# Two-layer encoder trunk: stored MLP operands converted three products behind their load at the seam of the two MLP products, and at most 22 halves in advance

## The chip, the cores and the metric

The kernel runs on one core of a Trainium2 chip. The metric is the device time of one execution in microseconds. TensorE multiplies, ScalarE (ACT) and VectorE (DVE) prepare operands and read results out of PSUM, GpSimd (POOL) does little here, SyncE (SP) issues most of the loads, and 16 DMA engines move the data.

## What is computed

Two layers on 1024 tokens of width 1024, in float32: a recurrent mixer and an MLP, then a shared key and value, chunked attention and a second MLP. The change touches the two MLPs:

```python
def sqrelu_mlp(hn, w1, w2):
    return jnp.square(jax.nn.relu(hn @ w1)) @ w2
...
    for layer in range(DEPTH):
...
        hn = modulate(rms_norm(h, norm2_g[layer]), sh2, sc2)
        h = h + g2[:, None, :] * sqrelu_mlp(hn, mlp_w1[layer], mlp_w2[layer])
```

`w1` is 1024 x 4096, `w2` is 4096 x 1024.

## The kernel before

**Precision.** Each float32 operand is split into a high and a low part of a faster type. ScalarE copies the high part (L204), VectorE subtracts it to get the low part (L208). Each tile product is three matmuls, high by high, high by low and low by high (L337 to L339).

**Seven products for eight.** Most of an MLP is done in blocks of 2 by 2 with seven block products instead of eight (the names B11, T1, T2, B22, B21, T3, T4 in `PROD`, numbered x = 0 to 6). The operands are sums of blocks. For the weights VectorE builds them from a loaded *quad* of tiles (L123), after which ScalarE and VectorE convert them. For the hidden activations the sums are built once (L1224) and all blocks are stored to DRAM (`hid`), from where the second product loads them again. One such *piece* holds two blocks of 128 x 512. Each block, once split into high and low, fills one tile and is called a half here; a name needs four of them for the four row groups that a pair of steps uses.

One product of `Quads.product` is 12 matmuls. x = 2 and 5 and 6 add onto the bank that x = 0 began, x = 3 onto that of x = 1. The bank has to be read before it is added to again. In the first product x = 0 to 2 are read by ScalarE (L1306), x = 3 to 5 by VectorE (L1308), x = 6 by ScalarE (L1235). In the second product all are read by VectorE (L1335).

**Order.** In the MLPs and their neighbourhood the order of each engine's instructions is the order in which the Python code issues them. `Stream` (the object `ws`) keeps the books. After the matmuls of a product come, in this order: the read, `flush` (low parts of conversions, at most four units, a half being one and a wide weight tile two), `after` (jobs that are due, changes of limits), then the clock `now` goes up by one and `pump` runs. `pump` first issues loads, as long as the number of *raw* tiles (loaded, not yet converted) is below `ns`. Then it takes the first item of each queue that is ready: "p" builds the sums of a quad, "w" converts weights, "a" converts stored pieces. With `early` set, the raw count falls as soon as the high part is issued. The low part is held back until the next `flush`, so that it stands behind the next read on VectorE. Seven raw tiles come from a ring (`ws`), the others from the 38 general tiles (`s`). A load physically starts when the engine that last used its tile is done with it. With `strict` set, sums of a quad first empty all held-back low parts.

An item is ready when `now` is at least `lag[kind]` past the value at which its load was issued and when its halves still fit: `live` halves plus the new one must not exceed `cap`. For "a", `live` falls by two after each product of every second step of the second product.

**The seam.** The first product ends with the row groups 14 and 15 done as a pair, the second begins with its steps s0 and s1 as a pair. The last product of a pair is carried into the next one. The products around the seam are numbered P0, P1, ... here; (15,0) is row group 15, x = 0:

| P | product | P | product | P | product | P | product |
|---|---|---|---|---|---|---|---|
| 0 | (14,0) | 8 | (15,3) | 16 | (15,6) | 24 | (s0,5) |
| 1 | (14,1) | 9 | (14,4) | 17 | (s1,0) | 25 | (s1,4) |
| 2 | (13,6) | 10 | (14,5) | 18 | (s1,1) | 26 | (s1,5) |
| 3 | (15,0) | 11 | (15,4) | 19 | (s0,2) | 27 | (s0,6) |
| 4 | (15,1) | 12 | (15,5) | 20 | (s0,3) | 28 | (s2,0) |
| 5 | (14,2) | 13 | (14,6) | 21 | (s1,2) | 29 | (s2,1) |
| 6 | (14,3) | 14 | (s0,0) | 22 | (s1,3) | 30 | (s1,6) |
| 7 | (15,2) | 15 | (s0,1) | 23 | (s0,4) | 31 | (s3,0) |

In the load order stand the pieces of B11 for row groups 0 to 3, the two weight quads of s0 and s1 (W0, W1), the pieces of T1, T2, B22, B21, T3 and T4 for the same row groups, B11 to B22 for groups 4 and 5, the quads of s2 and s3 (W2, W3), and so on. W3.0 is the first operand made from the quad W3. `reload` brings back the residual stream in between.

At P3 (row group 15, x = 0) the code sets `lag["p"]` to 2, at each product of group 15 it raises `cap["a"]`, and `ns` becomes 10 (L1317 to L1321). At P14 `lag["p"]` goes back to 4 (L1373, L1374), at P30 `ns` becomes 11 and `strict` ends (L1375, L1376). `lag["a"]` is 2 from the start of the program. `cap["a"]` keeps its last value until the end of the MLP. Layer 0 and layer 1 run the same code.

Of the kernel before, what the change touches and what calls it, by code (L numbers as in the profile page):

```python
# [311 lines left out]
def trunk(ctx: ExitStack, tc: tile.TileContext, I, out, dbg=None, stop=None):  # L312
# [12 lines left out]
    def slot(dt=F32, tag="a", shape=(128, 1024)):  # L325
        cnt[0] += 1
        return ap_.tile(list(shape), dt, name=f"s{cnt[0]}", tag=tag)
# [5 lines left out]
    def hs(half):  # L333
        return slice(half * HALF, (half + 1) * HALF)
# [29 lines left out]
    ws = Stream(nc, slot, whp, wsp)  # L364
# [839 lines left out]
    def mlp_body(l, h, nrm, nxt, last):  # L1204
        g2 = mods[l][:, 40:48]

        def store(p, ca, cb_):

            f = "p (a b) -> p a b"

            def squares():
                if l == 0 and p in (0, 1, 14, 15):
                    nc.scalar.dma_start(hid[p][:, 0:8:7], ca.rearrange(f, a=2))
                else:
                    nc.scalar.dma_start(hid[p][:, 0:1], ca[:, hs(0)].unsqueeze(1))
                nc.scalar.dma_start(hid[p][:, 3:5], cb_.rearrange(f, a=2))

            def sums():
                a, b = hs(0), hs(1)
                for out, in0, in1 in ((cb_[:, a], ca[:, b], cb_[:, a]),  # L1220
                                      (ca[:, b], ca[:, b], ca[:, a]),
                                      (ca[:, a], ca[:, a], cb_[:, a]),
                                      (cb_[:, b], cb_[:, b], ca[:, a])):
                    V.tensor_tensor(out=out, in0=in0, in1=in1, op=ALU.subtract)  # L1224

            def rest_():
                nc.scalar.dma_start(hid[p][:, 1:3], ca.rearrange(f, a=2))
                nc.scalar.dma_start(hid[p][:, 5:7], cb_.rearrange(f, a=2))

            for d, job in zip({12: (2, 3, 4), 13: (2, 3, 4), 14: (2, 16, 20), 15: (6, 18, 22)}.get(p, (2, 4, 8)),  # L1230
                              (squares, sums, rest_)):
                ws.at(d, job)

        def relu2(t, src=None):
            A_.activation(out=t, in_=t if src is None else src, func=AF.Relu)  # L1235
            A_.activation(out=t, in_=t, func=AF.Square)
# [53 lines left out]
        def reload(*ks):  # L1290
            for k in ks:
                h[k] = slot()
                nc.sync.dma_start(h[k], nrm.dram[k])
# [4 lines left out]
        def hidden(p):  # L1298
            ca, cb_ = slot(), slot()
            spots = (ca[:, hs(0)], cb_[:, hs(0)], ca[:, hs(1)], ca[:, hs(1)], ca[:, hs(0)],  # L1300
                     cb_[:, hs(0)], cb_[:, hs(1)])

            def read(x, ps, spots=spots):
                t = spots[x]
                if x < 3:
                    A_.activation(out=t, in_=ps, func=AF.Copy)  # L1306
                elif x < 6:
                    V.tensor_tensor(out=t, in0=t, in1=ps, op=ALU.add)  # L1308
                    ws.at(1, relu2, t)
                else:  # L1310
                    relu2(t, ps)

            def after(x, p=p, ca=ca, cb_=cb_):
                ws.run()
                if x == 6:
                    store(p, ca, cb_)
                if (p, x) == (15, 0):  # L1317
                    ws.lag["p"] = 2
                if p == 15:
                    ws.cap["a"] = min(24, 4 * x + 4)  # L1320
                    ws.ns = 10  # L1321
                    if x in (3, 5):
                        reload(x - 3, x - 2)

            return [ws.next() for _ in range(4)], 4, nrm.op, read, after
# [7 lines left out]
        def add(m, half, ps):  # L1333
            t = h[m][:, hs(half)]
            V.scalar_tensor_tensor(out=t, in0=ps, scalar=g2[:, m : m + 1], in1=t, op0=ALU.mult,  # L1335
                                   op1=ALU.add)
# [3 lines left out]
        def final():  # L1340
            while finals:
                m, half = finals.pop(0)
                if last is not None:
                    last(h, (m,), half)
                else:
                    nxt.sq(m, hs(half))
# [12 lines left out]
        def second(s):  # L1359
            m1, m2 = 2 * (s % 4), 2 * (s % 4) + 1  # L1360
            spots = ((m1, 0), (m2, 1), (m1, 1), (m1, 1), (m1, 0), (m2, 1), (m2, 0))

            def read(x, ps):
                final()
                add(*spots[x], ps)
                if s > 11 and x > 2:
                    finals.append(spots[x])

            def after(x):
                ws.run()  # L1370
                if x == 3 and s < 2:
                    reload(4 + 2 * s, 5 + 2 * s)
                if (s, x) == (0, 0):  # L1373
                    ws.lag["p"] = 4  # L1374
                if (s, x) == (1, 6):  # L1375
                    ws.ns, ws.strict = 11, False  # L1376
                if s == 14 and l == 0:
                    ws.live["a"] -= 4 * (NAMES[x][0] == "T")
                elif s % 2:
                    ws.live["a"] -= 2 if s < 14 else 4  # L1380

            return [ws.next() for _ in range(4)], 4, Operands(s // 2 * 2), read, after
# [483 lines left out]
```

## Time and profile before

| | us |
|---|---|
| median of 3 runs | 2317.44 (2315.03 to 2317.73) |
| profiled execution, its own time | 2313.97 |
| span of that execution | 2312.2 |
| MLP of layer 0: first and last L1308 or L1335 of it | about 526 to 1110 |
| MLP of layer 1 | about 1700 to 2312 |

The granted clock of TensorE is 0.997 over the span. A row of a group or a timeline names the source line, the engine, the operation, output and input, the size and the count. In the timeline the first number is the start from the span's beginning, the second the duration, and a bracket holds how long the engine stood idle before it and who released it. A row of the stretches gives the stretch, its length, the busy time of TensorE, its weight loads, VectorE, ScalarE and GpSimd, each with a count, then the granted clock, the share of the DMA engines and GB/s. Matmul ends are modelled, so the starts are the better measure.

### The profile page before, as it was taken

To read this page: it belongs to the slowest core of one execution; us is meant where nothing else is said; L and a number is where in the kernel's file an instruction comes from. 1 tells how busy PE (TensorE), PEld (TensorE's weight loads), DVE (VectorE), ACT (ScalarE), POOL (GpSimd) and SP (SyncE) were. 2 spreads that over 40 slices of the span, in tenths; PEclk is the share of its full clock that TensorE was granted. 3 is DMA by queue.
4 is the path that set the end of the run, shared out by engine and by line. 5 is a ranking of instruction groups with operands and counts; after the bars stand their busy time and mean duration, and the time that the engine had idled before them with its cause. 6 is when DMAs were issued, how large, how long until landed. Compare 5 with 4: busy or idle time off the path is not lost. (4 is left out here: it accounts for less than half of the span.)

```text
span 2312.2 us, 29207 instructions
## 1 busy us (share of the span) xinstructions
PE 2242.3 (97%) x10588; PEld 1862.5 (81%) x10588; DVE 1761.7 (76%) x2658; ACT 1241.0 (54%) x2138; POOL 256.2 (11%) x331
## 2 busy tenths in 40 slices
PE   4999999999999999999999999998999999999999
PEld 2878878878888788887888879997888888788887
DVE  8679889698877798887777639995396655798876
ACT  5587793375555643434443259995275555633332
POOL 0001000200000000000000248873200000000000
PEclk9999999999999999999999999999999999999999
DMA  8225457426666775456334200014113444875452
GB/s 321 73 70 147 144 164 271 175 83 246 250 232 219 277 256 163 146 164 214 96 110 133 91 10 11 10 54 148 69 51 146 150 150 170 279 247 173 144 161 96
DMA packets 140284, 353.33 MB, mean 153 GB/s; under 512 B 14604, under 2 KB 16780, under 8 KB 140140
## 3 DMA queue, kind: packets, MB, share of 16 engines
q1 hardware_dynamic: 115996, 275.83, 35.5%
q10 hardware_dynamic: 20240, 64.10, 7.2%
q0 software_dynamic: 3904, 11.54, 1.9%
q8 instruction: 83, 1.36, 0.2%
q14 instruction: 61, 0.50, 0.1%
HBM read 257.56 MB, written 82.31 MB: 147 GB/s over the span
## 5 line engine op out<-in xcount | busy, mean ns | idle before, releaser
L337 PE MATMUL b<-s,wh 128*128 128x512 f32 (+1 forms) x2532 | 994.0, 393 | 20.0 <-DVE s L1308 5.6
L338 PE MATMUL b<-s,wh 128*128 128x512 f32 (+1 forms) x2532 | 989.9, 391 | 9.2 <-DVE s L846 5.3
L339 PE MATMUL b<-s,wl 128*128 128x512 f32 x2296 | 897.0, 391 | 0.0
L337 PEld LDWEIGHTS b<-s,wh 128*128 128x128 f32 (+1 forms) x2532 | 475.3, 188 | 129.9 <-issue 8.0
L338 PEld LDWEIGHTS b<-s,wh 128*128 128x128 f32 (+1 forms) x2532 | 475.4, 188 | 115.5 <-DVE s L846 6.3
L339 PEld LDWEIGHTS b<-s,wl 128*128 128x128 f32 x2296 | 430.9, 188 | 92.6
L204 ACT ACTIVATE wh<-ws 128x1024 fp32r<-128x1024 f32 (+3 forms) x264 | 253.0, 971 | 348.2 <-PE b L338 152.9
L208 DVE TENSOR_TENSOR wl<-ws,wh 128x1024 fp32r<-128x1024 f32 (+1 forms) x216 | 262.8, 1220 | 65.6 <-ACT wh L204 61.8
L1335 DVE SCALAR_TENSOR_TENSOR s<-b,mod,s 128x512 f32<-128x512 f32 x221 | 163.4, 746 | 88.5 <-PE b L339 88.5
L337 PE MATMUL b<-wh,s 128*128 128x512 f32 x384 | 149.9, 390 | 0.0
L338 PE MATMUL b<-wl,s 128*128 128x512 f32 x384 | 149.4, 389 | 0.0
L339 PE MATMUL b<-wh,s 128*128 128x512 f32 x384 | 148.9, 389 | 0.0
L204 ACT ACTIVATE s<-ws 128x512 fp32r<-128x512 f32 x196 | 112.3, 620 | 57.5 <-DMA ws<-ygd 17.5
L1308 DVE TENSOR_TENSOR s<-s,b 128x512 f32<-128x512 f32 x84 | 57.0, 683 | 102.6 <-PE b L339 102.5
L208 DVE TENSOR_TENSOR s<-ws,s 128x512 fp32r<-128x512 f32 x196 | 125.2, 683 | 7.6 <-ACT s L204 7.5
L204 ACT ACTIVATE wh<-s 128x1024 fp32r<-128x1024 f32 (+1 forms) x52 | 50.4, 969 | 144.5 <-issue 45.9
L1573 POOL TENSOR_SCALAR dk<-s 128x1024 f32<-128x1024 f32 x16 | 18.6, 1162 | 833.2 <-DVE s L1513 830.6
L370 DVE CUSTOM_DVE_ANT_0 ws<-ws,cb,vec 128x1024 f32<-128x1024 f32 x58 | 73.7, 1279 | 31.3 <-DMA ws<-in_ada_dram 31.2
L1306 ACT ACTIVATE s<-b 128x512 f32<-128x512 f32 x84 | 50.0, 595 | 87.7 <-PE b L339 87.1
L339 PE MATMUL b<-s,wh 128*128 128x512 f32 x236 | 91.9, 389 | 0.0
L343 DVE TENSOR_TENSOR s<-b,s 128x384 fp32r<-128x384 f32 x144 | 82.6, 593 | 11.1 <-ACT s L342 10.6
L1647 POOL TENSOR_SCALAR s<-s,sm 128x640 f32<-128x640 f32 (+4 forms) x128 | 86.2, 685 | 22.6 <-DVE sm L1645 19.5
(168 smaller groups left out, 3108.8 us busy)
## 6 DMA issues: line engine op xcount, KB each, us to landing
hid<-s ACTq DMA_DIRECT2D x100, 512.0 KB, 4.0
ws<-in_w_dram SPq DMA_DIRECT2D x185, 256.0 KB, 3.4
ws<-hid SPq DMA_DIRECT2D x87, 512.0 KB, 4.1
ws<-in_ada_dram SPq DMA_DIRECT2D x56, 512.0 KB, 4.5
s<-hid SPq DMA_DIRECT2D x41, 512.0 KB, 5.9
s<-in_ada_dram SPq DMA_DIRECT2D x40, 512.0 KB, 7.4
s<-in_w_dram SPq DMA_DIRECT2D x51, 256.0 KB, 4.3
ws<-in_w_in_dram SPq DMA_DIRECT2D x22, 512.0 KB, 7.4
```

Source lines behind the costliest of these rows:

```text
L204: self.nc.scalar.activation(out=hi[:rows, :n], in_=src, func=AF.Copy)
L208: self.nc.vector.tensor_tensor(out=lo[:rows, :n], in0=src, in1=hi[:rows, :n].bitcast(F32), op=ALU.subtract)
L337: PE.matmul(ps, ah, bh, start=start, stop=False, skip_group_check=more)
L338: PE.matmul(ps, ah, bl, start=False, stop=False, skip_group_check=more)
L339: return PE.matmul(ps, al, bh, start=False, stop=stop, skip_group_check=more).ins
L343: V.tensor_tensor(out=lo, in0=src, in1=hi.bitcast(F32), op=ALU.subtract)
L370: V.tensor_tensor_reduce(out=t, in0=t, in1=cb, op0=ALU.mult, op1=ALU.add, scale=1.0, scalar=bias, accum_out=dst)
L1306: A_.activation(out=t, in_=ps, func=AF.Copy)
L1308: V.tensor_tensor(out=t, in0=t, in1=ps, op=ALU.add)
L1335: V.scalar_tensor_tensor(out=t, in0=ps, scalar=g2[:, m : m + 1], in1=t, op0=ALU.mult, op1=ALU.add)
L1573: G.tensor_scalar(out=d4, in0=s3.unsqueeze(2).broadcast_to([128, 8, 2, 64]), scalar1=1.0, scalar2=1.0, op0=ALU.mult, op1=ALU.mult)
L1647: G.tensor_scalar(out=p[:, lo:640], in0=p[:, lo:640], scalar1=sm[:, 4 + e : 5 + e], scalar2=1.0, op0=ALU.mult, op1=ALU.mult)
```

## The change

From P3 to P30 of each MLP a stored piece may be converted three steps of the clock after its load was issued, where two were enough before. From P12 on the limit of halves is 22, where it was 24; up to there it is the same (4 at P3, 8 at P4, 12 at P7, 16 at P8, 20 at P11).

```diff
                 if (p, x) == (15, 0):
-                    ws.lag["p"] = 2
+                    ws.lag["p"], ws.lag["a"] = 2, 3
                 if p == 15:
-                    ws.cap["a"] = min(24, 4 * x + 4)
+                    ws.cap["a"] = min(22, 4 * x + 4)
                     ws.ns = 10
...
                 if (s, x) == (1, 6):
-                    ws.ns, ws.strict = 11, False
+                    ws.ns, ws.strict, ws.lag["a"] = 11, False, 2
```

## The prediction

> **What bounds the kernel now.** I read the page's busy times first, then TensorE's timeline for gaps in the two second products, then what stood in front of each gap.
>
> ```profile
> span 2312.2 us, 29207 instructions
> PE 2242.3 (97%) x10588; PEld 1862.5 (81%) x10588; DVE 1761.7 (76%) x2658; ACT 1241.0 (54%) x2138; POOL 256.2 (11%) x331
> ```
>
> TensorE is the bound. The change can only win gaps of TensorE where the operands are prepared, or make new ones. Stretches around the seam of the two products, layer 0 then layer 1 (the clock, in the column behind POOL, is 1.00 throughout):
>
> ```profile
> 774.60:800.00 25.40, 22.22 (x97) 18.10 (x98) 19.82 (x30) 22.46 (x39) 0.00 (x0) 1.00 0.91 317
> 800.00:828.00 28.00, 27.58 (x121) 22.55 (x122) 25.85 (x37) 12.91 (x20) 0.00 (x0) 1.00 0.85 310
> 1992.70:2018.00 25.30, 22.28 (x97) 17.94 (x96) 19.66 (x29) 22.41 (x39) 0.00 (x0) 1.00 0.98 335
> 2018.00:2047.00 29.00, 27.92 (x122) 22.84 (x123) 26.85 (x39) 13.27 (x21) 0.00 (x0) 1.00 0.80 289
> ```
>
> Here TensorE idles, ScalarE is nearly full, and the DMA engines are 80 to 98% busy. TensorE's rows, the last two columns being the gap and its releaser:
>
> ```profile
> 737.48 0.39 PE L339 MATMUL b<-s,wl 128*128 128x512 f32 x1
> ...
> 740.20 0.39 PE L339 MATMUL b<-s,wl 128*128 128x512 f32 x1
> ...
> 776.81 0.50 PE L337 MATMUL b<-s,wh 128*128 128x512 f32 x1 [2.23 <-DVE s L1308]
> 799.87 0.47 PE L337 MATMUL b<-s,wh 128*128 128x512 f32 x1 [0.97 <-DVE s L1335]
> 816.86 0.47 PE L337 MATMUL b<-s,wh 128*128 128x512 f32 x1 [0.42 <-DVE s L1335]
> 1994.81 0.50 PE L337 MATMUL b<-s,wh 128*128 128x512 f32 x1 [1.93 <-DVE s L1308]
> 2018.06 0.47 PE L337 MATMUL b<-s,wh 128*128 128x512 f32 x1 [1.15 <-DVE s L1335]
> 2035.67 0.47 PE L337 MATMUL b<-s,wh 128*128 128x512 f32 x1 [1.03 <-DVE s L1335]
> ```
>
> The first two rows are 12 starts apart, so a product takes 2.72 us and a matmul starts every 0.227 though its row says 0.39. A gap therefore costs its bracket plus 0.16: 2.39, 1.13 and 0.58 in layer 0 (4.10), 2.09, 1.31 and 1.19 in layer 1 (4.59), **8.69 us** together. That is the most this change can win: 0.38% of the span. Counting 12 starts per product, the gaps stand before P13, P21 and P27. Each of these adds onto a PSUM bank that VectorE must have read after P10, P17 and P24.
>
> ScalarE's, VectorE's and SyncE's rows before the first gap (layer 1's first wait last):
>
> ```profile
> 769.30 0.98 SPq L163 DMA_DIRECT2D ws<-hid  x2
> ...
> 774.20 1.15 ACT L204 ACTIVATE s<-ws 128x512 fp32r<-128x512 f32 x2 [5.89 <-DMA ws<-hid]
> 775.54 1.15 ACT L204 ACTIVATE s<-ws 128x512 fp32r<-128x512 f32 x2 [0.19 <-DMA ws<-hid]
> ...
> 770.99 1.22 DVE L208 TENSOR_TENSOR wl<-ws,wh 128x1024 fp32r<-128x1024 f32 x1
> 774.86 1.29 DVE L208 TENSOR_TENSOR s<-ws,s 128x512 fp32r<-128x512 f32 x2 [2.65 <-ACT s L204]
> 776.07 0.68 DVE L1308 TENSOR_TENSOR s<-s,b 128x512 f32<-128x512 f32 x1
> ...
> 1992.20 1.15 ACT L204 ACTIVATE s<-ws 128x512 fp32r<-128x512 f32 x2 [4.74 <-DMA ws<-hid]
> ```
>
> The T1 pieces are issued at 769.30 and land at 774.20, 4.9 us later. Their conversion already stands at the head of ScalarE's queue, its low halves at the head of VectorE's, and behind those the read of P10 (776.07). P10 itself was over at 769.2, so TensorE waits for a read held up by a load. The second gap is the same backlog:
>
> ```profile
> 780.04 1.23 DVE L208 TENSOR_TENSOR wl<-s,wh 128x1024 fp32r<-128x1024 f32 x1 [1.49 <-ACT wh L204]
> 781.18 1.29 DVE L208 TENSOR_TENSOR s<-ws,s 128x512 fp32r<-128x512 f32 x2
> 782.39 0.68 DVE L1308 TENSOR_TENSOR s<-s,b 128x512 f32<-128x512 f32 x1
> 782.98 1.29 DVE L208 TENSOR_TENSOR s<-ws,s 128x512 fp32r<-128x512 f32 x2
> ...
> 788.56 1.23 DVE L208 TENSOR_TENSOR wl<-ws,wh 128x1024 fp32r<-128x1024 f32 x1 [2.55 <-ACT wh L204]
> ...
> 793.97 0.74 DVE L1335 SCALAR_TENSOR_TENSOR s<-b,mod,s 128x512 f32<-128x512 f32 x1
> 794.63 1.28 DVE L208 TENSOR_TENSOR s<-ws,s 128x512 fp32r<-128x512 f32 x2
> ...
> 798.98 0.74 DVE L1335 SCALAR_TENSOR_TENSOR s<-b,mod,s 128x512 f32<-128x512 f32 x1
> ...
> 815.97 2.06 DVE L1335 SCALAR_TENSOR_TENSOR s<-b,mod,s 128x512 f32<-128x512 f32 x3
> ```
>
> From the starts: a wide low part takes 1.14 us, two low halves 1.21, a read 0.59 (L1308) or 0.66 (L1335). The read of P17 comes at 798.98 and ends 799.7, where TensorE wanted it at 798.7.
>
> **The change part by part.** It adds and removes no instruction; it moves conversions. Pump n is the bookkeeping after product n. First I laid out before's order by the rules of the code (raw tiles at most 10, a conversion frees its raw tile and lets the next load in). Stored pieces are loaded in pumps 6, 8, 10, 12 and converted in 8 (4 halves), 10 (6), 12 (8), 14 (2): bursts, as ScalarE's rows have them. With a lag of 3 the same rules give pumps 9 (4 halves: T1), 11 (2: T2), 12 (4), 13 (2), 14 (2), 15 (4), and there the limit of 22 holds until P17 frees two.
>
> *First gap.* T1 moves to pump 9, so its low halves queue behind P10's read. That read follows the wide low part: 770.99 + 1.14 = 772.1, done 772.7. P13 can start at 776.81 − 2.39 = 774.42. The gap goes. The load is not moved, as it was held by its ring tile, not by a count. Next late on VectorE are T1's low halves, 774.86 to 777.4 as before, needed by P15 at 779.9; then reads of P11 and P12, done about 780.6, needed by P16 at 782.6.
>
> *Second gap.* From 780.6 to P17's read VectorE now has six pairs of halves (7.3), two wide parts (2.3) and three reads (2.0), 11.5 us, and I allow 2.4 for waiting on ScalarE: done 794.4. TensorE, 2.39 earlier, wants it at 774.42 + 8 × 2.72 = 796.2. T3's halves, in front of this read before, are now behind it. *Third gap.* Another 14 us of such work takes P24's read to 808.6, wanted at 812.5. Both go.
>
> *SyncE, ScalarE's queue and POOL.* A raw tile is held a product longer, but the issue waits for the low part that last read the tile, so issues stay within about 2 us of before's. The stores of the last two hidden parts sit on ScalarE's queue behind conversions that now wait less. POOL's column is 0.00 here. The 22 leaves one name less converted until the second product ends; each is still emitted three or more products before use.
>
> *What is late next.* Pieces waiting for the limit of 22 fill the raw tiles, so the next weight quads enter later. By the same count the last load of the second quad moves from pump 22 to 24 and its sums, four products on, from 26 to 28; its first operand, W3.0, is used by P31. Before's rows for it:
>
> ```profile
> 813.63 2.60 SPq L163 DMA_DIRECT2D s<-in_w_dram  x2
> ...
> 821.24 0.69 DVE L123 TENSOR_TENSOR s<-s 128x512 f32<-128x512 f32 x1 [2.01 <-DMA s<-in_w_dram]
> ...
> 823.90 0.74 DVE L1335 SCALAR_TENSOR_TENSOR s<-b,mod,s 128x512 f32<-128x512 f32 x1
> 824.57 1.21 DVE L208 TENSOR_TENSOR wl<-s,wh 128x1024 fp32r<-128x1024 f32 x1
> ```
>
> Sums take 2.66 us. Changed: P28 ends 817.9, its read 818.8, sums 821.4, read of P29 822.1, low part 823.3. P31 starts at 774.42 + 18 × 2.72 = 823.4 and needs it at its third matmul, 823.8. So the cost is nothing by 0.5 us of margin, if the load has landed by 818.8. If instead it lands no earlier than before (821.24, the DMA engines being full), the low part is there at 821.24 + 2.66 + 0.67 + 1.21 = 825.8 and P31 waits 1.9. Between 0 and 1.9 I take **1.0 per layer**, as the issue (about 813.7, after W2.0's low part) is near before's first. The Trainium skill, page "DMA: Bandwidth & Descriptors", section "Bandwidth", lists 0.95 us for 64 KB and 6.15 for 1 MB; my estimate from it for this quad's 512 KB is 3.4, which lands at 817.1, costs nothing and makes the sum −8.1 for the −6.1 below. The row of 769.30 took 4.9 for as much, so the trace does not bear that out here.
>
> For thin margins at P21 and P22 (1.8 and 1.5 us, with ScalarE waiting for loads) I take 0.3 per layer, between 0 and 1.3 (half of the old gaps there).
>
> Sum: −8.69 + 2 × 1.0 + 2 × 0.3 = **−6.1 us**. On the profiled execution (2313.97, span 2312.2) that is 2307.9; the median of the three runs is 3.5 above it, and the same step from it gives **2311.3**.
>
> **The rivals.**
> *The gap moves on.* TensorE gains 2.39 at P13, but if VectorE still reaches P17's read at 799.7, P21 starts where it did and all is given back: about 2317, range 2314.5 to 2319. For it: ScalarE is busy 22.46 of 25.40 us, and VectorE's brackets of 1.49 and 2.55 are waits for it. Against it: the 5.89 us that ScalarE stood still come back only where a load is not awaited, and 8 halves no longer come in one pump. Chance 0.25.
> *Half is given back to the weight quads*, or the lag only swaps waits: 1.9 per layer at P31 and some at P28, with 0.5 elsewhere: −3.4, 2314. Chance 0.10.
> *The smaller limit starves every pair (slower).* It holds at some seven changes of pair in each layer, 14 in all. If at each the second quad's sums slip past the first product of the next pair, its low part comes a read and a wide part late, 0.67 + 1.21 − 0.45 = 1.4 us: 14 × 1.4 = 19.9, less 8.7 won, +11: 2328.6. It decides where the sums start later than 819.3 on the clock above. Against it: from P30 on there are 11 raw tiles and a lag of 2, by which the count gives the order that before has at pumps 22 and 26, and that ran without a gap. The Trainium skill, "Perfetto Trace Analysis", section "Optimization Strategy", says repeated bubbles can mean too few buffers for the next tile; tiles held longer point that way. No repeated gap stands in the rows above. Chance 0.08.
>
> **How the numbers follow.** Forecast 0.57, own range 2307.5 to 2313; the others as given. 0.2%, about what a measurement of this kernel tells from no change, is 4.6 us: faster means below 2312.8. The forecast lies there but for 0.01, the next two do not: faster 0.56, same 0.36, slower 0.08. Leaving out the slower rival and the thin ends, the range is 2307.5 to 2317.8.
>
> **What would show it.** Right: no wait of some 5 us on a load before L204 of T1; L1308 before the low halves of T1; no gap before P13, P21, P27; the second quad's sums two products later, after P28; a gap of 0 to 2 us before P31. Wrong: a gap before P21 as large as the one won at P13 (the backlog was work, not waiting); waits for L208 or L123 at the third or fourth product of each later pair; or T1's conversion still ahead of P10's read.

## The result and the profile after

| | before | after |
|---|---|---|
| median of 7 runs each, side by side, us | 2314.49 (2311.82 to 2317.73) | 2306.84 (2305.20 to 2309.36) |
| ratio, 95% interval | 1 | 0.9968 [0.9956, 0.9979] |
| profiled execution: its own time, span | 2313.97, 2312.2 | 2305.20, 2303.1 |

The change takes 7.65 us off the medians, 4.9 to 10.2 by the interval. In the medians and ratios of this document one execution is left out, of the kernel cap_p17 below, which took 8093.11 us at a granted clock of 0.439. Top of the page of after, the span and the busy time by engine:

```profile
span 2303.1 us, 29191 instructions
...
PE 2238.9 (97%) x10588; PEld 1861.8 (81%) x10588; DVE 1760.6 (76%) x2658; ACT 1238.8 (54%) x2138; POOL 256.4 (11%) x331
```

Work and instruction counts of the compute engines are the same. What changed is idle time of TensorE, so the waits of TensorE are the view to read: engine, line, the line that it waited for, us in total, number, longest. First before, in layer 0 from P0 on (735 to 1060 us):

```profile
PE b L337 <- DVE s L1308: 2.2, 1, 2.2
PE b L337 <- DVE s L1335: 1.7, 3, 1.0
```

The same stretch of after:

```profile
PE b L339 <- DVE wl L208: 1.3, 2, 1.0
```

The waits for reads of PSUM (L1308, L1335) are gone in layer 0. In their place stand two shorter waits for the low half of a weight. After's rows of TensorE with a gap, layer 0 and then layer 1, last columns gap and releaser:

```profile
813.96 0.50 PE L339 MATMUL b<-s,wl 128*128 128x512 f32 x1 [0.97 <-DVE wl L208]
...
822.79 0.50 PE L339 MATMUL b<-s,wl 128*128 128x512 f32 x1 [0.38 <-DVE wl L208]
...
2012.34 0.50 PE L337 MATMUL b<-s,wh 128*128 128x512 f32 x1 [1.01 <-DVE s L1335]
...
2037.87 0.50 PE L339 MATMUL b<-s,wl 128*128 128x512 f32 x1 [0.26 <-DVE wl L208]
```

These are P28 and P31 in layer 0, P22 and P31 in layer 1. By the starts, which agree with the bracket plus 0.16 to 0.01, they cost 1.13, 0.54, 1.18 and 0.41 us, 3.3 together, against 8.69 before. No row with a gap is left before P13, P21 or P27.

Now VectorE in after, first at P10's read, then from P24's read on:

```profile
768.32 1.22 DVE L208 TENSOR_TENSOR wl<-ws,wh 128x1024 fp32r<-128x1024 f32 x1
769.45 0.68 DVE L1308 TENSOR_TENSOR s<-s,b 128x512 f32<-128x512 f32 x1
771.50 1.29 DVE L208 TENSOR_TENSOR s<-ws,s 128x512 fp32r<-128x512 f32 x2 [1.36 <-ACT s L204]
...
790.86 0.75 DVE L1335 SCALAR_TENSOR_TENSOR s<-b,mod,s 128x512 f32<-128x512 f32 x1
...
806.16 0.75 DVE L1335 SCALAR_TENSOR_TENSOR s<-b,mod,s 128x512 f32<-128x512 f32 x1
809.36 0.69 DVE L123 TENSOR_TENSOR ws<-s 128x512 f32<-128x512 f32 x1 [2.45 <-DMA s<-in_w_dram]
...
812.69 1.22 DVE L208 TENSOR_TENSOR wl<-ws,wh 128x1024 fp32r<-128x1024 f32 x1
...
817.54 0.74 DVE L1335 SCALAR_TENSOR_TENSOR s<-b,mod,s 128x512 f32<-128x512 f32 x1
818.21 0.68 DVE L123 TENSOR_TENSOR ws<-ws 128x512 f32<-128x512 f32 x1
...
821.52 2.35 DVE L208 TENSOR_TENSOR wl<-ws,wh 128x1024 fp32r<-128x1024 f32 x2
```

Two orders have changed. P10's read (769.45) stands ahead of T1's low halves (771.50). And the sums of the quad W2 (809.36) stand behind P24's read (806.16). They wait 2.45 us for their load, and P24's read, which P27 needs, is already out. What still stands behind them is the low half of W2.0 (812.69), and that makes the gap at P28. Before, the sums stood ahead of P24's read, which is the first of the three in the row of 815.97:

```profile
810.32 0.68 DVE L123 TENSOR_TENSOR s<-ws 128x512 f32<-128x512 f32 x1
```

How much of the time is the seam's? I take two durations per execution: from the read of P2 (L1235) to the last matmul of TensorE's run in layer 0's MLP (its start; the L337 after it, near 1062 to 1073, has a bracket of 1.5 or 1.7), and from the read of P2 in layer 1 to the end of the span. Together they are 666.6 us before and 660.8 after: **5.8 us**. Of the 9.1 us between the two spans another 2.8 lie ahead of P2 in layer 0 (that read starts at 747.42 before and 744.58 after), where both kernels issue the same instructions; that part is chance (the second trace of before below has that read at 745.46).

### The profile page after: what moved, and what is told of

Same layout as the page of the kernel before. It is cut to its first block, busy times and chain, and to the rows that moved or that the text cites. A ratio compares the mean times of both kernels' runs of the same rounds, so it can differ in the third digit from the quotient of the medians.

```text
span 2303.1 us, 29191 instructions
## 1 busy us (share of the span) xinstructions
PE 2238.9 (97%) x10588; PEld 1861.8 (81%) x10588; DVE 1760.6 (76%) x2658; ACT 1238.8 (54%) x2138; POOL 256.4 (11%) x331
## 5 line engine op out<-in xcount | busy, mean ns | idle before, releaser
L337 PE MATMUL b<-s,wh 128*128 128x512 f32 (+1 forms) x2532 | 992.0, 392 | 13.4 <-ACT s L842 6.3
L337 PEld LDWEIGHTS b<-s,wh 128*128 128x128 f32 (+1 forms) x2532 | 474.5, 187 | 119.9 <-ACT s L842 8.7
L208 DVE TENSOR_TENSOR wl<-ws,wh 128x1024 fp32r<-128x1024 f32 (+1 forms) x222 | 270.1, 1221 | 52.8 <-ACT wh L204 49.3
L1335 DVE SCALAR_TENSOR_TENSOR s<-b,mod,s 128x512 f32<-128x512 f32 x221 | 164.0, 748 | 86.4 <-PE b L339 86.4
L337 PE MATMUL b<-wh,s 128*128 128x512 f32 x384 | 149.9, 390 | 0.0
L204 ACT ACTIVATE s<-ws 128x512 fp32r<-128x512 f32 x208 | 117.4, 618 | 48.0 <-DMA ws<-ygd 17.3
L1308 DVE TENSOR_TENSOR s<-s,b 128x512 f32<-128x512 f32 x84 | 57.2, 684 | 106.3 <-PE b L339 95.3
L208 DVE TENSOR_TENSOR s<-ws,s 128x512 fp32r<-128x512 f32 x208 | 133.5, 685 | 6.1 <-ACT s L204 6.1
```

What stands on the lines that cost most here:

```text
L204: self.nc.scalar.activation(out=hi[:rows, :n], in_=src, func=AF.Copy)
L208: self.nc.vector.tensor_tensor(out=lo[:rows, :n], in0=src, in1=hi[:rows, :n].bitcast(F32), op=ALU.subtract)
L337: PE.matmul(ps, ah, bh, start=start, stop=False, skip_group_check=more)
```

## The experiments

Theories at the start. *Lag*: the lag of 3 wins the time and the limit of 22 only costs some; the prediction reasoned so. *Limit*: the lag only moves the gap on to a later product, and the limit does the rest. All kernels below differ from before or after only in lines of the seam and compute the same. Each of the three groups of kernels had its own executions of before: medians 2316.21 (21 runs), 2315.99 (27) and 2315.48 (23).

All results in one table. Gaps are taken from the starts (bracket plus 0.16, to 0.01) at the product named, layer 0 / layer 1; "seam" is the sum of the two durations above, in the profiled execution, us:

| kernel | median | ratio to before, 95% | gaps | seam |
|---|---|---|---|---|
| before | | | P13 2.38, P21 1.13, P27 0.58, P41 0.45 / P13 2.09, P21 1.31, P27 1.19 | 666.6 |
| before_again | one execution, 2314.89 | | P13 1.86, P21 3.01 / P13 1.56, P21 1.52, P27 0.99, P41 1.48 | 669.3 |
| after | 2306.84 | 0.9968 [0.9956, 0.9979] | P28 1.13, P31 0.54 / P22 1.18, P31 0.41 | 660.8 |
| both_again | 2306.45 | 0.9956 [0.9942, 0.9971] | P28 1.56, P31 0.52 / P22 1.00, P28 0.23, P31 0.54 | 661.5 |
| lag_only | 2316.24 | 1.0001 [0.999, 1.0012] | P22 0.50, P27 4.76 / P27 3.87 | 670.0 |
| cap_only | 2310.02 | 0.9973 [0.9963, 0.9982] | P13 1.89, P28 0.66, P31 0.52 / P13 1.19 | 663.0 |
| both_ns11 | 2307.41 | 0.996 [0.9948, 0.9973] | P22 0.85, P27 1.24, P41 0.69 / P22 0.80, P27 1.25, P41 0.46 | 662.5 |
| lag_p6 | 2318.53 | 1.0009 [1.0, 1.0018] | P28 0.34, P31 4.11 / P22 0.38, P28 0.61, P31 4.11 | 671.4 |
| p6_only | 2322.94 | 1.0029 [1.002, 1.0038] | P13 1.02, P21 1.99, P31 4.10 / P13 1.76, P31 4.11 | 673.6 |
| lag_p64 | 2313.45 | 0.9987 [0.9978, 0.9997] | P22 0.85, P28 0.61, P31 0.53, P41 2.79 / P31 1.14, P41 2.77 | 668.7 |
| both_p2 | 2319.73 | 1.0014 [1.0003, 1.0024] | P27 6.76 / P27 3.59 | 671.1 |
| cap_p17 | 2316.07 | 0.9996 [0.9986, 1.0007] | P13 2.74, P27 1.03, P41 0.34 / P13 1.71, P21 0.85, P27 4.23 | 670.4 |
| both_reload | 2304.05 | 0.9942 [0.9929, 0.9956] | none / none | 656.8 |
| best | 2301.53 | 0.9933 [0.9919, 0.9946] | none / none | 656.6 |

### One part of the change at a time

lag_only keeps the limit of 24; cap_only keeps the lag of 2; both_again is the changed kernel once more and before_again a second trace of before.

```diff
 lag_only, against before
-                    ws.lag["p"] = 2
+                    ws.lag["p"], ws.lag["a"] = 2, 3
...
-                    ws.ns, ws.strict = 11, False
+                    ws.ns, ws.strict, ws.lag["a"] = 11, False, 2
 cap_only, against before
-                    ws.cap["a"] = min(24, 4 * x + 4)
+                    ws.cap["a"] = min(22, 4 * x + 4)
```

> The lag of 3 from P3 to P30, the limit left at 24. Theory (the lag wins the gaps of TensorE before P13, P21 and P27; the limit of 22 fills raw tiles and so makes the two gaps before the low parts of P28 and P31, 1.2 and 0.6 us in layer 0, 0.5 at P31 in layer 1): the gap before P13 stays away, the sums of the second quad come after P26 again, the gaps of P28 and P31 are gone, and the time is 1 to 2.5 us below that with both edits, 0.40% below before. Rival (the limit of 22 earns its place by keeping T3's last halves behind the reads of P17 and P18): a gap of 1 us or more before P21 or P22 in both layers, time equal to both edits or up to 2 us above it.

> The limit of 22, the lag left at 2. Theory: the gap before P13 stays as before (2.4 and 2.1 us), the one before P21 shrinks by at most 1.2 us as two halves fewer are converted in front of it, P28 and P31 get gaps of 0.5 to 1.5 us: time within 0.15% of before. Rival (the limit alone thins out the backlog): the gaps before P21 and P27 go and the time is more than 0.15% below before.

> The changed kernel once more, beside the others on one chip. Every theory: 0.2 to 0.4% below before; the gaps of the seam as in its first trace, that is 1.8 us in layer 0 and 1.8 us in layer 1 in place of 4.3 and 4.7. If the gaps come and go between executions, they are chance and not the order.

> The kernel before once more, for a second trace of it. Theory (the gaps follow from the order): P13, P21 and P27 have the same gaps to 0.3 us in both layers, while the gap of 1.7 us at 630 us, in code that the change does not touch, and the first 60 us may differ. Rival (a good part of the 9.1 us between the two first traces is chance): the gaps before P13, P21 and P27 move by 1 us or more.

The lag alone wins nothing (1.0001), which neither side of its expectation had. The limit alone wins 6.2 us (2316.21 − 2310.02), as its rival had it, and both 9.8. before_again goes against its theory too: the same kernel moved by 1.9 us at P21 of layer 0, so the size of a single gap is partly chance. lag_only does remove the gap before P13, and also that before P21. But TensorE then arrives earlier at P27 and waits there; its rows around P27:

```profile
816.15 0.77 PE L337 MATMUL b<-s,wh 128*128 128x512 f32 x1 [4.61 <-DVE s L1335]
...
817.14 0.63 PE L339 MATMUL b<-s,wh 128*128 128x512 f32 x1
...
820.75 0.40 PE L339 MATMUL b<-s,wh 128*128 128x512 f32 x1
```

The matmul is released by a read on VectorE. VectorE of lag_only shows what that read stood behind:

```profile
809.60 0.69 DVE L123 TENSOR_TENSOR s<-ws 128x512 f32<-128x512 f32 x1 [1.52 <-DMA ws<-in_w_dram]
...
812.26 0.75 DVE L1335 SCALAR_TENSOR_TENSOR s<-b,mod,s 128x512 f32<-128x512 f32 x1
...
815.26 2.06 DVE L1335 SCALAR_TENSOR_TENSOR s<-b,mod,s 128x512 f32<-128x512 f32 x3
```

W2's sums wait 1.52 us for the load of their quad. P24's read, the first of the three at 815.26, follows the sums, the read of P23, W2.0's low part and a pair of halves: 6.32 us from the start of the sums to its end (809.60 to 815.26 + 0.66). In cap_only the same sums start behind P24's read:

```profile
808.91 0.75 DVE L1335 SCALAR_TENSOR_TENSOR s<-b,mod,s 128x512 f32<-128x512 f32 x1
812.29 0.69 DVE L123 TENSOR_TENSOR ws<-s 128x512 f32<-128x512 f32 x1 [2.63 <-DMA s<-in_w_dram]
```

They wait even longer (2.63) and TensorE has no gap at P27. The gap before P13 stays in cap_only, 1.89 and 1.19. both_again doesn't have it, and its six executions (up to 2307.67) all lie below the nine of cap_only (from 2307.94), 3.6 us by the medians. But it has 2.7 us more than cap_only at P28 of layer 0 and at P22, P28 and P31 of layer 1, and the two seams differ by only 1.5 (663.0, 661.5). So the lag wins its gap where the limit keeps P27 clear; how much of it is kept, 1.5 to 3.6 us, stays open.

### Is it the place of the sums, or that their load is awaited?

both_ns11 gives the changed kernel one more raw tile from x = 5 of row group 15 on, so that W2's load goes out earlier. lag_p6 and p6_only leave the limit at 24 and hold the quads' sums back by `lag["p"]` instead; lag_p6 has the lag of 3 for stored pieces, p6_only the lag of 2. lag_p64 does that for W2 alone.

```diff
 both_ns11, against after
-                    ws.ns = 10
+                    ws.ns = 11 if x > 4 else 10
 lag_p6, against lag_only (p6_only: the same for lag["p"], against before)
-                    ws.lag["p"] = 4
+                    ws.lag["p"] = 6
...
-                    ws.ns, ws.strict, ws.lag["a"] = 11, False, 2
+                    ws.ns, ws.strict, ws.lag["a"], ws.lag["p"] = 11, False, 2, 4
 lag_p64, against lag_only
-                    ws.lag["p"] = 4
+                    ws.lag["p"] = 6
+                if (s, x) == (0, 5):
+                    ws.lag["p"] = 4
```

> Both edits, and one raw tile more from P12 on (11 instead of 10), so that the loads of the second-product quads enter one conversion earlier and their sums go back from P24 and P28 to P22 and P26. Theory now (the limit of 22 wins because it puts the sums of W2, which wait for their load, behind the read of P24 on VectorE): the gap before P27 of 4 to 5 us is back in both layers, as with the lag alone, and the time is within 0.15% of before. Rival (the limit wins because two halves fewer stand on VectorE and ScalarE before P17 and P24; the place of the sums costs only the gaps of P28 and P31): no gap of over 1 us before P27, the gaps of P28 and P31 gone, 0.40 to 0.55% below before.

> The lag of 3 with the limit left at 24, and the sums of a quad six products behind their load instead of four from P14 to P30, which puts them after P24 and P28 as with both edits. Theory (place of the sums): the gap before P27 is gone, the time is that of both edits to 0.1% or better, 0.40 to 0.50% below before, as the load of W2 enters two products earlier and the gap at P28 shrinks under 0.5 us. Rival (number of halves): the gap before P27 stays above 3 us and the time is that of the lag alone.

> The kernel before with nothing but the sums six products behind their load from P14 to P30. Theory (place of the sums): the gap before P13 stays at 1.5 to 2.4 us, the gap before P27 goes, the one before P21 stays at up to 3 us as T3's last halves are still in front: 0.10 to 0.27% below before. Rival (number of halves): nothing won, within 0.1% of before.

> As the lag of 3 with the limit of 24 and sums six products behind, but four again from P24 on: the sums of W2 after P24, those of W3 after P26. Theory: no gap of over 1 us before P27 or P28, the gap of 0.5 us at P31 gone too, 0.40 to 0.55% below before, 0.5 to 2 us below both edits. Rival: as for the kernel with six throughout.

**both_ns11** puts the sums back to where lag_only has them, but with the load landed. Its rows on VectorE, the first the read of P22:

```profile
804.24 0.75 DVE L1335 SCALAR_TENSOR_TENSOR s<-b,mod,s 128x512 f32<-128x512 f32 x1
...
806.10 0.69 DVE L123 TENSOR_TENSOR s<-ws 128x512 f32<-128x512 f32 x1
...
811.77 2.06 DVE L1335 SCALAR_TENSOR_TENSOR s<-b,mod,s 128x512 f32<-128x512 f32 x3
```

The sums start without a bracket, 3.50 us sooner than in lag_only (806.10 for 809.60), and the way to the end of P24's read is as long as there (6.33 us). P27 starts at 812.66 after a gap of 1.24, so TensorE was there at 811.4; in lag_only it was there at 816.15 − 4.76 = 811.4 too. The gap is smaller by 3.52 where the sums are earlier by 3.50. But not all of the 3.50 is the load. VectorE of lag_only is late already at the read of P22:

```profile
806.13 0.75 DVE L1335 SCALAR_TENSOR_TENSOR s<-b,mod,s 128x512 f32<-128x512 f32 x1
```

That is 1.89 later (806.13 for 804.24); most of it arises between the reads of P17 and P19, where lag_only has a pair of low halves more than both_ns11, which also has the lower limit. So of lag_only's 4.76 us, 1.24 remain with the load landed, about 1.6 is the wait for the load (the bracket of 1.52), and 1.9 is other work of VectorE in front. The expectation had a gap of 4 to 5 us back with the sums, its rival none above 1; it came out between, and the time (0.996) is no different from after's. SyncE shows why lag_only's load is late; in both_ns11 three of the quad's four loads are issued at 798.84:

```profile
798.84 2.60 SPq L163 DMA_DIRECT2D ws<-in_w_dram  x3
```

In lag_only they go out 3.7 us later; SyncE waited 4.4 us there for a low part on VectorE that still had to read the raw tile:

```profile
802.52 2.47 SPq L163 DMA_DIRECT2D ws<-in_w_dram  x3
```

**lag_p6** and **p6_only** keep 24 and move the sums behind P24's read by their own lag. The gap before P27 goes in both, so the sums' place alone clears P27, without fewer halves. But both lose more at P31, which neither theory nor rival had; a row of ScalarE in lag_p6:

```profile
821.40 0.63 ACT L204 ACTIVATE s<-ws 128x512 fp32r<-128x512 f32 x1 [5.43 <-PE b L339]
```

And rows of VectorE in lag_p6:

```profile
822.06 0.69 DVE L208 TENSOR_TENSOR s<-ws,s 128x512 fp32r<-128x512 f32 x1 [3.64 <-ACT s L204]
822.67 0.75 DVE L1335 SCALAR_TENSOR_TENSOR s<-b,mod,s 128x512 f32<-128x512 f32 x1
823.33 0.68 DVE L123 TENSOR_TENSOR s<-ws 128x512 f32<-128x512 f32 x1
```

With 24 halves a conversion is issued so far ahead that its target is still being read by TensorE (5.43 us). Its low half (822.06) stands in front of P28's read (822.67) and so of W3's sums; these start at 823.33, and TensorE waits for W3.0's high part and then for its low part, 4.1 us in each layer. That the order was right at P27 and the time still not better (1.0009) is a miss for "move the sums and that is all". In after no row of ScalarE waits for TensorE between 811 and 824 in layer 0. That the limit is what prevents it was not tested by itself; lag_p64 avoids the wait with 24 halves.

**lag_p64** brings W3's sums four products behind their load again and loses only 0.53 and 1.14 at P31, but the next pair then has the old order at P41, 2.79 and 2.77. VectorE of lag_p64 before that gap:

```profile
848.02 0.69 DVE L123 TENSOR_TENSOR ws<-ws 128x512 f32<-128x512 f32 x1
...
853.68 1.40 DVE L1335 SCALAR_TENSOR_TENSOR s<-b,mod,s 128x512 f32<-128x512 f32 x2
```

Again the read that TensorE waits for ends 6.3 us (853.68 + 0.66 − 848.02) after the start of the sums of a quad. Why that quad's turn falls there in this kernel was not followed up. The win is 0.13%, for 0.40 to 0.55 expected.

### The place taken back, the limit taken back, and what is left

both_p2 is the changed kernel with `lag["p"]` of 2 instead of 4 from P14 to P30, which puts W2's sums back ahead of P24's read. cap_p17 has the limit of 22 only up to P16. both_reload is the changed kernel with the reloads of s0 and s1 one step of x later, that is, after P23 and P25 where they came after P20 and P22. best adds to it that W3's sums come one product earlier.

```diff
 both_p2, against after
-                    ws.lag["p"] = 4
+                    ws.lag["p"] = 2
...
-                    ws.ns, ws.strict, ws.lag["a"] = 11, False, 2
+                    ws.ns, ws.strict, ws.lag["a"], ws.lag["p"] = 11, False, 2, 4
 cap_p17, against before
-                    ws.cap["a"] = min(24, 4 * x + 4)
+                    ws.cap["a"] = min(22, 4 * x + 4)
...
+                if (s, x) == (1, 0):
+                    ws.cap["a"] = 24
 both_reload, against after
-                if x == 3 and s < 2:
+                if x == 4 and s < 2:
                     reload(4 + 2 * s, 5 + 2 * s)
 best, against both_reload
+                if (s, x) == (0, 5):
+                    ws.lag["p"] = 3
...
-                    ws.ns, ws.strict, ws.lag["a"] = 11, False, 2
+                    ws.ns, ws.strict, ws.lag["a"], ws.lag["p"] = 11, False, 2, 4
```

> Both edits, with the sums of a quad two products behind their load instead of four from P14 to P30: the sums of W2 go back in front of the reads of P23 and P24 (after P22 instead of P24), all else as with both edits. Theory A (the limit of 22 takes away the gap before P27 because it puts the sums, which wait for their load, behind the read of P24): a gap of 2 to 5 us before P27 in both layers, 0 to 0.2% below before. Theory B (it does so by fewer halves, or by tiles that come free earlier, wherever the sums stand): no gap of over 1.3 us before P27, 0.3 to 0.45% below before.

> The kernel before with the limit at 22 up to P16 and at 24 from P17 on: T3's last halves stay behind the read of P17, but the loads of W2 come early again and its sums stand after P22. Theory A: the gap before P13 as before, the one before P21 gone or under 0.5 us, a gap of 1 to 5 us before P27, time within 0.15% of before. Theory B: the gap before P27 stays away as with the limit alone, 0.2 to 0.3% below before.

> Both edits, and the four reloads of the residual stream one step of their x later (after P23 and P25 instead of P20 and P22), behind the loads of W2. Theory (the gap before P28's low part is the load of W2 landing late behind 2 MB of reloads): W2's sums wait under 1 us for their load, the gap at P28 falls from 1.1 to 1.6 us to under 0.3 us in layer 0, that at P31 stays at 0.4 to 0.6 us, 0 to 1.5 us below both edits. Rival (the DMA engines are full, whatever the order): the gap at P28 stays above 0.8 us, or a read of P28 waits for its reloaded tile and makes a gap of its own.

> As the kernel with the later reloads, and from P24 to P30 the sums three products behind their load, so that those of W3 come after P27 instead of P28. Theory: the gap at P31 goes too, 1 to 3 us below both edits (0.05 to 0.13%), no gap left from P13 to P40 but the one before P22. Rival: the sums then wait for W3's load on VectorE in front of the read of P28 and the gap at P31 stays or grows.

**both_p2** has the lag of 3 and the limit of 22, and yet the gap before P27 is back. VectorE of both_p2:

```profile
812.55 0.69 DVE L123 TENSOR_TENSOR ws<-s 128x512 f32<-128x512 f32 x1 [5.60 <-DMA s<-in_w_dram]
...
818.21 0.75 DVE L1335 SCALAR_TENSOR_TENSOR s<-b,mod,s 128x512 f32<-128x512 f32 x1
```

And its TensorE at P27, layer 0 and layer 1:

```profile
819.11 0.76 PE L337 MATMUL b<-s,wh 128*128 128x512 f32 x1 [6.60 <-DVE s L1335]
...
2037.98 0.47 PE L337 MATMUL b<-s,wh 128*128 128x512 f32 x1 [3.43 <-DVE s L1335]
```

The load wait of 5.60 us is now TensorE's, and the ratio is 1.0014, slightly above the 0 to 0.2% below before that theory A had. The load lands at nearly the same point of the seam as in after: 812.55 and 809.36 are 65.2 and 64.8 us behind the reads of P2 (747.32, 744.58). After's own rows give about the same gap. Its P28 starts at 812.38, hence P27 at 812.38 − 2.72 = 809.66; with the sums first, P24's read would end at 809.36 + 6.32 = 815.7, a gap of some 6 us, where after has none.

**cap_p17** keeps the limit only until P17. Layer 0 loses its gap before P21 and layer 1 has 0.85 of 1.31 left, but P27 is at 1.03 and 4.23, since with 24 W2's sums are early again (810.59, ahead of P24's read at 816.25); the time is no different from before's (0.9996). So with the lag of 2 the limit clears the two gaps at two different times: P21 before P17, whose read then has one pair of low halves fewer in front, and P27 after it.

**both_reload** tests what the limit costs. In after, SyncE issues two reloads of the residual (L1293) between the loads of the quad W2 (L163, the last of them the two at 798.90), and two more (803.03) behind the first load of W3 (802.35):

```profile
797.92 0.89 SPq L1293 DMA_DIRECT2D s<-hsp  x2
798.90 1.75 SPq L163 DMA_DIRECT2D s<-in_w_dram  x2
802.35 0.33 SPq L163 DMA_DIRECT2D ws<-in_w_dram  x1
803.03 2.07 SPq L1293 DMA_DIRECT2D s<-hsp  x2
```

In both_reload all of W2's loads are ahead of them, and VectorE's wait for the quad is 1.57 us for 2.45 (under 1 was expected):

```profile
806.61 0.75 DVE L1335 SCALAR_TENSOR_TENSOR s<-b,mod,s 128x512 f32<-128x512 f32 x1
808.93 0.69 DVE L123 TENSOR_TENSOR ws<-s 128x512 f32<-128x512 f32 x1 [1.57 <-DMA s<-in_w_dram]
...
812.26 1.22 DVE L208 TENSOR_TENSOR wl<-ws,wh 128x1024 fp32r<-128x1024 f32 x1
```

Counted from P2's read, W2.0's low half comes 2.1 us earlier (812.26 − 746.23 for 812.69 − 744.58). The gaps of P28 and P31 are gone, that of P31 against the expectation, and the seam takes 656.8 us for after's 660.8. The view of TensorE's waits is empty for both_reload and for **best**, in layer 0 from 735 to 1060 us and in layer 1 from 1957 on. best is the lowest of all, 13.95 us below before by the medians of its group and 0.9933 [0.9919, 0.9946]; its five executions (2300.52 to 2303.32) all lie below the seven of after (from 2305.20) and the six of both_again (from 2304.22). Between both_reload and best the intervals overlap, and their seams differ by 0.2 us, so what W3's sums add to the reloads stays open.

## Why the prediction was right in part

**The step was right, the anchor was not.** The forecast step of −6.1 us lies inside the measured −4.9 to −10.2, and the seam itself took 5.8 us less. The forecast time of 2311.3 was 4.5 too high (3.0 from the median it starts at, 2317.44 − 2314.49, and 1.5 from the step) and the range's low end of 2307.5 was 0.7 too high: the measured 2306.84 lies outside. The step that failed is "the median of the three runs is 3.5 above it, and the same step from it gives 2311.3". The median of three, 2317.44, was itself high: with more executions before had 2314.49, 2316.21, 2315.99 and 2315.48. Seven executions of before spread over 5.9 us, about as much as the step itself, and three of them place the median no better than to a few us. The low end is not worked out anywhere. It stood just 0.4 below the other estimate of the same paragraph, 2307.9 from the profiled execution; with the two costs at their own lower bounds of nothing, the sum is −8.69 and that execution gives 2305.3.

**"8.69 us, the most this change can win".** Right as a reading of one execution, wrong as a bound. It leaves out the 0.45 before P41 of the same execution, which after no longer has. In the second trace of before P21 alone cost 3.01, with a slower clock behind it, and the seam took 2.7 us more. The gaps of 8.69 were one draw.

**First gap.** Right, step by step. The prediction has P10's read done at 772.7. After's clock is 2.84 ahead at P2; on before's clock its read ends at 769.45 + 0.59 + 2.84 = 772.9. The gap goes in every kernel with the lag of 3 and stays in every one without it.

**Second gap.** Right in time: P17's read was to be done at 794.4, and is at 790.86 + 0.66 + 2.84 = 794.4. That T3's halves pass behind this read was laid to the conversions held by the limit of 22. cap_only (both layers) and cap_p17 (layer 0) bear that out. But lag_only has no gap at P21 either, so each part clears it by itself there, in the executions that were profiled.

**Third gap: right outcome, wrong reason, so luck.** "Another 14 us of such work takes P24's read to 808.6": measured 806.16 + 0.66 + 2.84 = 809.7, and no gap. But the step did not say what was in front of the read. It counted work and neither the wait for W2's load nor that W2's sums change their place, which decides it (both_p2 against after, lag_p6 against lag_only). The forecast put the limit's later quads down as a cost only ("what is late next"). In fact more than half of the win comes with the limit (6.2 of 9.8 us in one group): later sums are sums behind P24's read.

**The first rival, "the gap moves on"**, with a chance of 0.25, is what the lag alone does: 2316.24 for its "about 2317", only at P27 where the rival had P21.

**The costs.** P31 was to wait 1.0 per layer; it waits 0.54 and 0.41. W3's sums do move behind P28's read (817.54, 818.21) and find their load landed, as the lower end of that bound had it. The page of the Trainium skill quoted there, "DMA: Bandwidth & Descriptors", section "Bandwidth", gave −8.1 by an estimate that lets the load land in time. Its table is of transfers issued from GpSimd and gives the busy time of the DMA engines, where these loads are SyncE's. W3's load did land in time here, issued by 809.4 and used at 818.21, so no row shows how long it took; the gaps at P31 came from VectorE's backlog instead. Missing in the sum was P28, 1.13 (1.56 in both_again), which only the second rival names, without a size: W2's load too goes out late and, as both_reload shows, behind the reloads. The 0.3 per layer for thin margins came out as 0 and 1.18 (P22 of layer 1). There ScalarE waited for two stored pieces; rows of ScalarE in after:

```profile
2004.40 1.15 ACT L204 ACTIVATE s<-ws 128x512 fp32r<-128x512 f32 x2 [1.50 <-DMA ws<-hid]
...
2007.11 1.15 ACT L204 ACTIVATE s<-ws 128x512 fp32r<-128x512 f32 x2 [1.55 <-DMA ws<-hid]
```

No experiment was made on that gap alone; it is absent in both_reload and best, and stays open. All terms together: −8.69 + 3.26 = −5.4 by the gaps, −5.9 with P41, for −6.1 forecast and 5.8 measured on the seam. So the forecast step came out near the traces with P31 too large and P28 left out, which is in part luck.

**The slower rival**, every pair starved, did not come: after has no wait of TensorE in the later pairs of either layer. (Its 14 × 1.4 is 19.6, not 19.9.)

## What to carry to other kernels

On an engine that works in order, ask of each piece of preparation what it may have to wait for and which read of PSUM stands behind it: in this kernel work that depends on a load belonged behind the reads that TensorE needed next, even if that made it later, as long as its own result was not late (P28, and P31 of lag_p6). Follow an early gain to the next such place before counting it; here what the lag won at P13 and P21 was lost at P27 until the other edit moved what stood there. And anchor a forecast of a few tenths of a per cent on the spread of the executions: the median of three was 1 to 3 us above those of 7 to 27.

## What was not expected of the hardware

After a long gap TensorE does not restart at full rate. In lag_only's rows above, after a gap of 4.61 us, the durations are 0.63 until about 820.1 and 0.40 after it, with the granted clock at 0.50; between 817.14 and 819.70 matmuls start 0.43 us apart for 0.227 otherwise. Three stretches of lag_only; the clock is the third column from the end:

```profile
812.00:816.00 4.00, 0.00 (x0) 0.00 (x0) 4.00 (x7) 1.63 (x3) 0.00 (x0) 0.70 1.04 414
816.00:820.00 4.00, 3.85 (x9) 3.14 (x10) 3.48 (x7) 0.23 (x1) 0.00 (x0) 0.50 1.03 387
820.00:824.00 4.00, 4.00 (x18) 3.22 (x18) 3.93 (x6) 2.30 (x3) 0.00 (x0) 0.94 0.11 39
```

Some nine matmuls at 0.2 us more each add about 1.8 us to a gap, which no wait shows. It happened after shorter gaps too; TensorE in before_again at P21:

```profile
799.24 0.55 PE L337 MATMUL b<-s,wh 128*128 128x512 f32 x1 [2.85 <-DVE s L1335]
...
800.01 0.63 PE L339 MATMUL b<-s,wl 128*128 128x512 f32 x1
...
803.41 0.40 PE L339 MATMUL b<-s,wl 128*128 128x512 f32 x1
```

Here a gap of 2.85 was enough, and eight starts were slow. Near this length it goes either way: after lag_p64's bracket of 2.63 at P41 five starts came at full rate and eight then at 0.42 to 0.43, after cap_p17's 2.59 at P13 all came at 0.22 to 0.24 but the first. After before's 2.23 none was slow. Two shorter gaps close together count too: at P31 of lag_p6 brackets of 1.76 and 2.03, two matmuls apart, were followed by ten starts at 0.42 to 0.43 in each layer. The Trainium skill, "TensorE: Matmul & The Clock Gate", section "What's actually happening", has the clock halved after an idle window of about 3.4 us and back after a busy one of as much, and calls the window free-running. The slow stretch here, 816.2 to 820.1, and the changing start of it agree with that; the gaps of 2.63 and 2.85 and the pair of 1.76 and 2.03 are below its figure, and there the measurement decides. So in this kernel a gap of 3.0 us cost 4.6 (before_again at P21: 2.85 + 0.16 and eight starts of 0.2 more), and that is a part of why lag_only, lag_p6 and both_p2 give back all that they win.
